# Stores of the RWKV mixers moved to ScalarE's and GpSimd's queues, a shorter first inverse, and later places for the fronts of the chunks

## The chip, the cores and the metric

The kernel runs on one core of one Trainium2 chip. The metric is the time of one execution on the device in microseconds; the median of three runs is taken. Beside the times there is a profile of one execution, which tells for every engine when each instruction ran and what it waited for. The engines are named as the profile names them: PE is TensorE (matrix multiplies; PEld is its loading of weights), DVE is VectorE, ACT is ScalarE, POOL is GpSimd, and SP is SyncE, which here does nothing but issue DMAs. ACT and POOL can issue DMAs too, from the same queue of instructions in which their arithmetic stands.

## The reference, cut to what matters

One inference step of two layers over 1048 tokens (16 meta tokens, 1024 prompt tokens, 8 decode tokens), model width 1024, all in float32. Layer 0 is a Conformer convolution and an MLP; layer 1 is an RWKV-7 mixer and an MLP. The mixer makes six mixtures of each token with the one before it, projects them, and runs a recurrence per head of 64:

```python
r = (xr @ w_r); k = (xk @ w_k); v = (xv @ w_v)
w_log = -softplus(-(w0 + tanh(xw @ w1) @ w2)) - 0.5
decay = exp(-exp(w_log));  a = sigmoid(a0 + (xa @ a1) @ a2);  g = sigmoid(xg @ g1) @ g2
# per head, token after token:
sa = einsum('bhvk,bhk->bhv', S, -kk_t)
S = S * w_t + sa[..., None] * (kk_t * a_t) + v_t[..., None] * k_t
y = einsum('bhvk,bhk->bhv', S, r_t)
# then a norm per head, the bonus (r * k * r_k) * v, the gate g, and @ w_o
```

## The kernel before, in words

The kernel goes through layer 0 first, then the mixer of layer 1, then its MLP. This case is about the mixer.

*Groups and places.* The tokens are cut into four groups (`G1`: 272, 256, 256 and 264 tokens). `mixer_in(g)` goes over the model width in eight places `p` of 128 channels each. At each place PE projects `r`, the small gates `l_g`, `l_w`, `l_a` and `v`, and, one place late, the keys `k` of the next group; ACT copies the results out of PSUM and applies the nonlinear functions, DVE makes from them the operands of the recurrence (`ab`). Before the places, `gate` and `decay_rate` multiply the whole group by narrow weights (`p_g`, `p_wa`, L943 and L944), and `tail` ends the last place of the group before.

*Through DRAM.* What one part makes and another reads in another layout goes through DRAM: the keys (`d_k`), the gates (`d_g`), the operands of the recurrence (`d_ab`), the values with tokens on the partitions (`d_v`), the small matrices to be inverted (`d_n`) and their inverses (`d_p`), the bonus (`d_bv`) and the recurrence's outputs (`d_y`). Before the change SP's queue issues nearly all these stores, and all loads of weights and operands as well.

*Chunks.* The recurrence is computed in chunks of 64 tokens: chunk 0 holds the 16 meta tokens, chunks 1 to 16 the prompt, four for each group. `inverses(c, n)` (L1139 on) inverts small triangular matrices of 32 rows for `n` chunks at once on DVE: it loads `ni` from `d_n`, does 30 steps of one multiply and one add (L1151, L1152), and stores to `d_p`. It is run once for chunk 0 and once for each group's four chunks, during the next group. `front(c)` loads a chunk's operands, makes `A`, the products within the chunk, and transposes the loaded inverse on DVE (`x32`, L1203). `chunk(c)` goes on with the small products `gg`, `W`, `po`, `U`, `S` and `Y` on PE and updates the state `sv`.

*What sets the order.* The program is traced in order; a planner then orders the instructions of each engine by its own estimate, but not PE's: inside `manual_schedule` PE runs in the order in which the program was traced. So PE waits at an instruction whose input is late, even where later ones could run. Inverses and chunks are Python generators. The mixer calls `tick(g)` seven times at each place (five times in group 3). Each call takes one step of the current inverse (`invert`), adds 2.0 to a credit in groups 1 to 3 and runs the recurrence until its yields (costs, in `RW`) have used the credit up (`advance`), and takes one step of the norm of the first output group. A chunk may begin when `st["inv"]` says that its inverse has been traced. `step(c + 1)` lets the next chunk's front run within a chunk, for no credit, if its inverse has been traced.

*Behind the mixers* come the output projection and MLP of the first output group (`mixer_out`, `mlp`). They are traced with what is left of the recurrence, the decode step and the remaining norms as fill, called some 208 times. The last chunk transposes its state on PE (`pfs`, L1310) and stores it.

Of the kernel before, what the change touches and what calls it, by code (L numbers as in the profile page):

```python
# [16 lines left out]
P = 128  # L17
# [3 lines left out]
META = 16  # L21
# [6 lines left out]
HS = 64  # L28
# [17 lines left out]
HALF = [slice(0, HS), slice(HS, P)]  # L46


def hybrid_step(tc, x_prompt, x_sample, state_conv, state_shift, state_wkv, meta_tokens,
# [8 lines left out]
    nc = tc.nc  # L58
    ctx = ExitStack()
    with ctx:  # L60
# [16 lines left out]
        d_k = dram.tile([P, KT, T], F32, name="d_k")  # L77
        d_ab = dram.tile([NCH, P, KT, 2, 2 * HS], F32, name="d_ab")
        d_v = dram.tile([NCH * HS, D], F32, name="d_v")
# [790 lines left out]
        def keys(g, fill):  # L870

            c0, n = G1[g]
            nm = lambda s, *a: f"{s}{g}" + "".join(f"_{x}" for x in a)
            mix = prep[g][0]
            act = [mix(2, k) for k in range(KT)]
            pn = bank(nm("pn"), "x")
            add_pn = lambda: None

            def to_pn(p, sq):
                return lambda: nc.tensor.matmul(pn[:, :n], head_sel(p), sq[:, :n], start=p == 0, stop=p == KT - 1)  # L880
            for p in range(KT):
                yield
                ps = proj(next(wrkv), act, n, nm("k", p), fill)
                k_ = pr.tile([P, N1], F32, name=nm("st", p), tag="st", bufs=2)
                nc.scalar.copy(k_[:, :n], ps[:, :n])
                nc.sync.dma_start(d_k[:, p, c0:c0 + n], k_[:, :n])
                sq = pr.tile([P, N1], F32, name=nm("sq", p), tag="rk", bufs=2)
                nc.scalar.activation(sq[:, :n], ps[:, :n], AF.Square, scale=vec("k_k", p))
                add_pn()
                add_pn = to_pn(p, sq)  # L890
            r16 = lorap.tile([P, N1], F32, name=nm("r16"), tag="lf")
            r16p = norm[g] = [lorap.tile([P, N1], F32R, name=nm("r16" + q), tag="r16" + q, bufs=2)[:, :n] for q in "hl"]
            add_pn()
            nc.vector.tensor_scalar(r16[:, :n], pn[:, :n], L2_EPS * L2_EPS, None, op0=ALU.max)
            nc.scalar.activation(r16[:, :n], r16[:, :n], AF.Sqrt)
            nc.vector.reciprocal(r16[:, :n], r16[:, :n])
            split(*r16p, r16[:, :n], nc.vector)
        carry = {"tail": lambda: None}

        def mixer_in(g, tick):  # L900
# [51 lines left out]
            def decay_rate(ws):  # L952
                ps = narrow(ws, "wa")
                nc.scalar.activation(lwa[0][HALF[0], :n], ps[HALF[0]], AF.Tanh)
                nc.scalar.copy(lwa[1][HALF[1], :n], ps[HALF[1]])
# [23 lines left out]
            wg, ww = narrow_w(1, "g"), narrow_w(0, "wa")  # L979
            act = mixed(0)  # L980
            gate(wg)
            decay_rate(ww)
            carry["tail"]()
            act_v = mixed(3)
            r16p = norm.pop(g)
# [2 lines left out]
            def finish(p, rk, ab, vv):  # L988
                def trace():
                    for s in segs:  # L990
                        if s[3] == HS:
                            nc.sync.dma_start(d_ab[s[0], :, p].rearrange("c r i x -> r c (i x)"),
                                              ab[:, s[4]:s[4] + s[2]].rearrange("r c i t -> r c (i t)"))
                        else:
                            nc.sync.dma_start(d_ab[0, :, p].rearrange("r i (j t) -> r (i j) t", j=2)[:, :, :s[3]],
                                              ab[:, s[4], :, :s[3]])

                    pv_ = bank(nm("vt", p))
                    vt = pr.tile([P, 2, P], F32, name=nm("vt", p), tag="vt")
                    pieces = [(i, a0 + i * P, P) for i in range(ncg // 2)] + ([(2, 0, META)] if g == 0 else [])  # L1000
                    for i, c1, w in pieces:
                        nc.tensor.transpose(pv_[:w, i * P:(i + 1) * P], vv[:, c1:c1 + w], ident)
                    fs_ = slice(p * P, (p + 1) * P)
                    nc.scalar.copy(vt[:, :2].rearrange("p i x -> p (i x)"), pv_[:, :2 * P])
                    nc.sync.dma_start(d_v[ch0 * HS:(ch0 + ncg) * HS, fs_].rearrange("(i t) x -> t i x", t=P), vt[:, :2])
                    if g == 0:
                        vm = pr.tile([P, 2, P], F32, name=nm("vm", p), tag="vt")
                        nc.scalar.copy(vm[:META, 0], pv_[:META, 2 * P:3 * P])
                        nc.sync.dma_start(d_v[:META, fs_], vm[:META, 0])

                    n32 = pr.tile([P, 5, 32], F32, name=nm("n32", p), tag="n32", bufs=2)
                    if g == 0:
                        nc.gpsimd.memset(n32[:, 4], 0.0)
                    pn_ = bank(nm("nn", p))
                    for c in range(ncg):
                        for q in range(2):
                            for j in range(2):
                                o, js = 64 * q + 32 * j, slice(32 * j, 32 * j + 32)
                                nc.tensor.matmul(pn_[o:o + 32, c * 32:(c + 1) * 32], ab[HALF[q], c, 2, js], ab[HALF[q], c, 0, js],
                                                 start=True, stop=True, tile_position=(64 * q, o))  # L1020
                    nc.vector.tensor_mul(n32[:, :ncg], pn_[:, :ncg * 32].rearrange("p (c t) -> p c t", t=32),
                                         nmask.unsqueeze(1).broadcast_to([P, ncg, 32]))
                    if g == 0:
                        pm = bank(nm("nm", p))
                        tok = [slice(64 * q, 64 * q + META) for q in range(2)]
                        for q, o in enumerate(tok):
                            nc.tensor.matmul(pm[o, :META], ab[HALF[q], 4, 2, :META], ab[HALF[q], 4, 0, :META],
                                             start=True, stop=True, tile_position=(64 * q, 64 * q))
                        for o in tok:
                            nc.vector.tensor_mul(n32[o, 4, :META], pm[o, :META], nmask[o, :META])  # L1030
                    nc.sync.dma_start(d_n[ch0:ch0 + ncg, p].rearrange("c r t -> r c t"), n32[:, :ncg])
                    if g == 0:
                        nc.sync.dma_start(d_n[0, p], n32[:, 4])
                    pb = bank(nm("pk", p))
                    nc.tensor.matmul(pb[:, :n], hsum, rk[:, :n], start=True, stop=True)
                    bv = t_("bv", p, "bv", 2)
                    nc.vector.tensor_mul(bv[:, :n], vv[:, :n], pb[:, :n])
                    return lambda: nc.sync.dma_start(d_bv[:, p, c0:c0 + n], bv[:, :n])
                return trace

            def fetch(p):
# [5 lines left out]
            for p, rk2 in ahead_of(fetch):  # L1047
                both()
                ps = proj(next(wrkv), act, n, nm("r", p), both)
                nc.scalar.copy(rk2[:, 2, :n], ps[:, :n])  # L1050
                if npr < n:
                    dd(p, 4, rk2[:, 2, npr:n])
                ps = lora2(wg2, p, lg, f"g{p}")
                gt = t_("gt", p, "gt", 2)
                nc.scalar.copy(gt[:, :n], ps[:, :n])
                nc.sync.dma_start(d_g[:, p, c0:c0 + n], gt[:, :n])

                wa = pr.tile([P, 3, N1], F32, name=nm("wa", p), tag="wa", bufs=2)
                nav, am, cum = (wa[:, i, :] for i in range(3))
# [80 lines left out]
        def inverses(c, n):  # L1140


            B = n * 32
            blocks = lambda d: d[c:c + n].rearrange("c k (e s) t -> (c k e) s t", s=32)
            ni = wk.tile([P, 32, 32], F32, name=f"ni{c}", tag="ni")[:B]
            nc.sync.dma_start(ni, blocks(d_n))
            yield 5
            for j in range(30, 0, -1):
                wd = 31 - j
                o = wk.tile([P, 256], F32, name=f"tt{c}_{j}", tag="tt")[:B, :j * wd].rearrange("p (s t) -> p s t", t=wd)  # L1150
                nc.vector.tensor_mul(o, ni[:, :j, j:j + 1].broadcast_to([B, j, wd]), ni[:, j:j + 1, j + 1:].broadcast_to([B, j, wd]))  # L1151
                nc.vector.tensor_add(ni[:, :j, j + 1:], ni[:, :j, j + 1:], o)  # L1152
                if j % 4 == 0:
                    yield 1.5
            nc.gpsimd.memset(ni.rearrange("p s t -> p (s t)")[:, 0:1024:33], 1.0)
            nc.sync.dma_start(blocks(d_p), ni)
            yield 1
            st["inv"] = c + n - 1

        RW = [4.0, 2.4, 3.12, 5.0, 5.0, 1.28, 3.12, 0.8, 3.0]  # L1160
# [54 lines left out]
        def chunk(c):  # L1215
# [67 lines left out]
            if c > 0:  # L1283
# [10 lines left out]
                nc.scalar.copy(flat(yt), py)  # L1294
                t0 = META + (c - 1) * HS
                for q in range(2):
                    nc.sync.dma_start(d_y[t0:t0 + HS].rearrange("t (k q v) -> q t k v", q=2, v=HS)[q], yt[HALF[q]])

            fs = w_([P, KT, HS], "fs", c, "w1")
            nc.vector.tensor_mul(fs, kv(ps), wend.broadcast_to([P, KT, HS]))  # L1300
# [2 lines left out]
                    nc.vector.tensor_add(sv[HALF[q], :, q, :], fs[HALF[q]], sw[HALF[q]])  # L1303
            else:
                nc.vector.tensor_add(fs, fs, sw)
                fo = w_([P, KT, HS], "fo", c, "sw")
                pt = bank("pfs", "w")
                for p in range(KT):
# [332 lines left out]
```

## Time and profile before

| | us |
|---|---|
| median of three runs | 2875.47 |
| lowest and highest | 2875.14 and 2879.01 |
| the profiled execution | 2871.15 |
| its span, first to last instruction | 2869.4 |
| mean granted clock of PE | 0.967 |

How to read it: the profile gives the busy time of each engine, and for each idle stretch the instruction that ended it. A wait is written as the waiting instruction, an arrow, and what released it: an engine with the tile and the line, or a DMA with what it carried. "x" is a count. In a timeline the columns are start and duration in microseconds, engine, line, operation, tiles, shape. In a table of stages a stretch is given with its length, the busy time of each engine with its number of instructions, the granted clock of PE, and the busy share and rate of the DMA engines. SP's own rows are issues of DMAs: their duration is the time that the queue was taken up by issuing, not that of the transfer. The mixers of groups 0 to 3 lie between about 1163 and 1878 us of the span.

### The profile page before, as it was taken

What the parts mean: (1) busy time and instruction counts of PE and PEld (TensorE: products, weight loads), DVE (VectorE), ACT (ScalarE), POOL (GpSimd) and SP (SyncE); (2) the same over time, 40 slices, a digit from 0 to 9 for tenths busy, and PEclk for the clock granted to TensorE, in tenths of its full rate; (3) what the DMA queues carried; (4) which work ended last, traced back from release to release, by engine and by line L of the source; (5) the groups of instructions that cost most, each with busy time, mean ns of one, the idle gap of its engine ahead of it and who ended that gap; (6) DMA issues with size and microseconds to landing.
All of it is one profiled execution on the core that took longest, in us unless ns stands there. A gap on an engine that the chain in (4) does not pass through costs nothing.

```text
span 2869.4 us, 51630 instructions
## 1 busy us (share of the span) xinstructions
PE 2672.5 (93%) x19594; PEld 2526.5 (88%) x19594; DVE 1799.4 (63%) x3618; ACT 1188.2 (41%) x2235; POOL 1433.1 (50%) x1983
## 2 busy tenths in 40 slices
PE   8999999999999899996998897987889999999998
PEld 7999999999999898885786786877889999999998
DVE  5999999995455545345656464477995554443444
ACT  5545444544354342332454453445444453222223
POOL 6677878987788774000010010154658773333332
PEclk9999999999999999998999899988999999999999
DMA  6663544454445643676677566776665542222221
GB/s 175 178 185 90 153 136 132 138 179 135 139 130 162 183 139 105 192 215 170 173 172 203 140 180 156 179 199 152 175 195 171 170 144 83 67 74 67 67 60 41
DMA packets 651959, 416.43 MB, mean 145 GB/s; under 512 B 126440, under 2 KB 600616, under 8 KB 651710
## 3 DMA queue, kind: packets, MB, share of 16 engines
q1 hardware_dynamic: 645468, 410.20, 50.6%
q10 hardware_dynamic: 6018, 2.89, 0.4%
q8 instruction: 155, 2.54, 0.4%
q14 instruction: 94, 0.77, 0.1%
q0 software_dynamic: 224, 0.03, 0.0%
HBM read 345.60 MB, written 68.37 MB: 144 GB/s over the span
## 4 chain that ended last, share of the span: by engine, by line
PE 72%; DVE 12%; DMA 6%; POOL 3%; issue 3%; ACT 3%; SPq 0%; DVEq 0%; ACTq 0%; POOLq 0%
PE out L187 7%; PE out L189 7%; PE out L188 7%; PE ps_in L187 7%; PE ps_in L189 7%; PE ps_in L188 7%; PE pk L865 4%; PE pv L865 3%; PE pr L865 3%; DVE cv L519 1%; POOL wo_lo L162 1%; DVE tt L1151 1%; POOL wi_lo L162 1%; DVE ni L1152 1%; PE A L1189 1%
## 5 line engine op out<-in xcount | busy, mean ns | idle before, releaser
L162 POOL TENSOR_TENSOR wo_lo<-wo_raw,wo_hi 128x256 fp32r<-128x256 f32 x736 | 563.8, 798 | 274.0 <-ACT wo_hi L157 267.5
L162 POOL TENSOR_TENSOR wi_lo<-wi_raw,wi_hi 128x256 fp32r<-128x256 f32 x640 | 487.2, 793 | 294.8 <-ACT wi_hi L157 290.9
L187 PE MATMUL out<-hh,wo_hi 128*128 128x352 f32 (+2 forms) x1536 | 504.5, 328 | 25.7 <-DVE h L355 14.4
L355 DVE TENSOR_TENSOR h<-h,out 128x352 f32<-128x352 f32 (+2 forms) x768 | 387.4, 510 | 196.6 <-PE out L189 196.1
L189 PE MATMUL out<-hl,wo_hi 128*128 128x352 f32 (+2 forms) x1536 | 495.6, 325 | 7.5 <-DVE hl L141 7.5
L187 PE MATMUL ps_in<-m_h,wi_hi 128*128 128x352 f32 (+2 forms) x1536 | 495.2, 323 | 1.7 <-DVE h L355 1.7
L188 PE MATMUL out<-hh,wo_lo 128*128 128x352 f32 (+2 forms) x1536 | 496.6, 323 | 0.0
L189 PE MATMUL ps_in<-m_l,wi_hi 128*128 128x352 f32 (+2 forms) x1536 | 494.0, 322 | 1.2 <-DVE m_l L285 1.2
L188 PE MATMUL ps_in<-m_h,wi_lo 128*128 128x352 f32 (+2 forms) x1536 | 492.1, 321 | 0.0
L519 DVE SCALAR_TENSOR_TENSOR cv<-u,wdw,cv 128x352 f32<-128x352 f32 (+2 forms) x720 | 376.4, 572 | 0.7
L157 ACT CAST wi_hi<-wi_raw 128x1024 fp32r<-128x1024 f32 x160 | 168.0, 1050 | 393.6 <-PE out L189 200.2
L187 PEld LDWEIGHTS out<-hh,wo_hi 128*128 128x128 f32 x1536 | 293.8, 191 | 32.7 <-DVE h L355 17.2
L157 ACT CAST wo_hi<-wo_raw 128x1024 fp32r<-128x1024 f32 x184 | 192.6, 1049 | 306.2 <-PE out L189 154.3
L189 PEld LDWEIGHTS out<-hl,wo_hi 128*128 128x128 f32 x1536 | 292.6, 191 | 9.5 <-DVE hl L141 9.4
L188 PEld LDWEIGHTS out<-hh,wo_lo 128*128 128x128 f32 x1536 | 293.0, 191 | 0.7
L187 PEld LDWEIGHTS ps_in<-m_h,wi_hi 128*128 128x128 f32 x1536 | 289.8, 189 | 3.5 <-issue 2.2
L189 PEld LDWEIGHTS ps_in<-m_l,wi_hi 128*128 128x128 f32 x1536 | 288.5, 188 | 2.6 <-DVE m_l L285 1.8
L188 PEld LDWEIGHTS ps_in<-m_h,wi_lo 128*128 128x128 f32 x1536 | 288.8, 188 | 1.0
L342 DVE SCALAR_TENSOR_TENSOR r<-ps_in,rs_m 128x352 f32<-128x352 f32 (+2 forms) x192 | 98.2, 514 | 238.1 <-PE ps_in L189 234.5
L141 DVE TENSOR_TENSOR hl<-s,hh 128x352 fp32r<-128x352 f32 (+2 forms) x192 | 147.4, 769 | 108.0 <-ACT hh L140 107.8
L344 ACT ACTIVATE s<-r 128x352 f32<-128x352 f32 (+2 forms) x192 | 93.8, 491 | 134.7 <-DVE r L342 131.6
L865 PE MATMUL pv<-mx,wv_raw 128*128 128x256 f32 (+2 forms) x512 | 126.3, 395 | 8.2 <-ACT rk L1050 6.8
(350 smaller groups left out, 4810.6 us busy)
## 6 DMA issues: line engine op xcount, KB each, us to landing
wi_raw<-in_w_mlp_in_dram SPq DMA_DIRECT2D x160, 512.0 KB
wo_raw<-in_w_mlp_out_dram SPq DMA_DIRECT2D x160, 512.0 KB
wk_raw<-in_rwkv_w_k_dram SPq DMA_DIRECT2D x32, 512.0 KB
wr_raw<-in_rwkv_w_r_dram SPq DMA_DIRECT2D x32, 512.0 KB
wv_raw<-in_rwkv_w_v_dram SPq DMA_DIRECT2D x32, 512.0 KB
d_ab<-ab SPq DMA_DIRECT2D x32, 512.0 KB
pg_raw<-in_conv_w_pw_dram SPq DMA_DIRECT2D x24, 512.0 KB
pa_raw<-in_conv_w_pw_dram SPq DMA_DIRECT2D x24, 512.0 KB
```

The source lines that it names most:

```text
L141: eng_lo.tensor_sub(lo, src, hi.bitcast(F32))
L157: nc.scalar.copy(hi[:, :a * b], raw[:, :a * b])
L162: eng_lo.tensor_sub(lo[:, cs], raw[:, cs], hi[:, cs].bitcast(F32))
L187: nc.tensor.matmul(ps, w[0], act[0], start=first, stop=False)
L188: nc.tensor.matmul(ps, w[1], act[0], start=False, stop=False)
L189: nc.tensor.matmul(ps, w[0], act[1], start=False, stop=last)
L342: nc.vector.scalar_tensor_tensor(r[:, :n], ps[:, :n], 0.0, rs()[:, :n], op0=ALU.max, op1=ALU.mult)
L344: nc.scalar.activation(s[:, :n], r[:, :n], AF.Square)
L355: nc.vector.tensor_add(hv[:, 4 * i + m, :], hv[:, 4 * i + m, :], ps[:, :n])
L519: nc.vector.scalar_tensor_tensor(acc[m][:, :n], ug[:, m, j:j + n], wdw[:, m, j:j + 1], acc[m][:, :n], op0=ALU.mult, op1=ALU.add)
L865: nc.tensor.matmul(ps[:, :n], w[:, k, :], act[k], start=k == 0, stop=k == KT - 1)
L1151: nc.vector.tensor_mul(o, ni[:, :j, j:j + 1].broadcast_to([B, j, wd]), ni[:, j:j + 1, j + 1:].broadcast_to([B, j, wd]))
```

## The change: what it does

1. In the mixers the stores of `d_k`, `d_v`, `d_g` and `d_y` are issued by ACT, those of `d_ab`, `d_n`, `d_bv` and `d_p` by POOL. SP keeps the loads (and, elsewhere in the kernel, the stores that it had).
2. `decay_rate`, the multiplication by the second narrow weight, is traced after the `r` projection of place 0 instead of ahead of `tail`.
3. The inverse of chunk 0 takes 14 steps over 16 rows instead of 30 over 32.
4. `inverses` yields 3 times (chunk 0) or 7 times (the others) after its store, instead of once, before it sets `st["inv"]`.
5. The last chunk yields once more ahead of the transposes of its state.

```diff
@@ keys
-                nc.sync.dma_start(d_k[:, p, c0:c0 + n], k_[:, :n])
+                nc.scalar.dma_start(d_k[:, p, c0:c0 + n], k_[:, :n])
@@ mixer_in
             gate(wg)
-            decay_rate(ww)
             carry["tail"]()
@@ mixer_in, finish (the stores of d_ab, the second of d_v, both of d_n likewise)
-                            nc.sync.dma_start(d_ab[s[0], :, p].rearrange("c r i x -> r c (i x)"),
+                            nc.gpsimd.dma_start(d_ab[s[0], :, p].rearrange("c r i x -> r c (i x)"),
...
-                    nc.sync.dma_start(d_v[ch0 * HS:(ch0 + ncg) * HS, fs_].rearrange("(i t) x -> t i x", t=P), vt[:, :2])
+                    nc.scalar.dma_start(d_v[ch0 * HS:(ch0 + ncg) * HS, fs_].rearrange("(i t) x -> t i x", t=P), vt[:, :2])
...
-                    return lambda: nc.sync.dma_start(d_bv[:, p, c0:c0 + n], bv[:, :n])
+                    return lambda: nc.gpsimd.dma_start(d_bv[:, p, c0:c0 + n], bv[:, :n])
@@ mixer_in, the places
                 nc.scalar.copy(rk2[:, 2, :n], ps[:, :n])
+                if p == 0:
+                    decay_rate(ww)
...
-                nc.sync.dma_start(d_g[:, p, c0:c0 + n], gt[:, :n])
+                nc.scalar.dma_start(d_g[:, p, c0:c0 + n], gt[:, :n])
@@ inverses
-            for j in range(30, 0, -1):
-                wd = 31 - j
+            top = META if c == 0 else 32
+            for j in range(top - 2, 0, -1):
+                wd = top - 1 - j
...
-                nc.vector.tensor_add(ni[:, :j, j + 1:], ni[:, :j, j + 1:], o)
+                nc.vector.tensor_add(ni[:, :j, j + 1:top], ni[:, :j, j + 1:top], o)
                 if j % 4 == 0:
                     yield 1.5
             nc.gpsimd.memset(ni.rearrange("p s t -> p (s t)")[:, 0:1024:33], 1.0)
-            nc.sync.dma_start(blocks(d_p), ni)
-            yield 1
+            nc.gpsimd.dma_start(blocks(d_p), ni)
+            for _ in range(3 if c == 0 else 7):
+                yield 1
             st["inv"] = c + n - 1
@@ chunk
-                    nc.sync.dma_start(d_y[t0:t0 + HS].rearrange("t (k q v) -> q t k v", q=2, v=HS)[q], yt[HALF[q]])
+                    nc.scalar.dma_start(d_y[t0:t0 + HS].rearrange("t (k q v) -> q t k v", q=2, v=HS)[q], yt[HALF[q]])
...
                 nc.vector.tensor_add(fs, fs, sw)
+                yield RW[7] + 3
                 fo = w_([P, KT, HS], "fo", c, "sw")
```

More of the change, by code (lines that the diff above doesn't have):

```diff
@@ L991, in trace @@
                         if s[3] == HS:
-                            nc.sync.dma_start(d_ab[s[0], :, p].rearrange("c r i x -> r c (i x)"),
+                            nc.gpsimd.dma_start(d_ab[s[0], :, p].rearrange("c r i x -> r c (i x)"),
                                               ab[:, s[4]:s[4] + s[2]].rearrange("r c i t -> r c (i t)"))
                         else:
-                            nc.sync.dma_start(d_ab[0, :, p].rearrange("r i (j t) -> r (i j) t", j=2)[:, :, :s[3]],
+                            nc.gpsimd.dma_start(d_ab[0, :, p].rearrange("r i (j t) -> r (i j) t", j=2)[:, :, :s[3]],
                                               ab[:, s[4], :, :s[3]])
@@ L1008, in trace @@
                         nc.scalar.copy(vm[:META, 0], pv_[:META, 2 * P:3 * P])
-                        nc.sync.dma_start(d_v[:META, fs_], vm[:META, 0])
+                        nc.scalar.dma_start(d_v[:META, fs_], vm[:META, 0])
                     n32 = pr.tile([P, 5, 32], F32, name=nm("n32", p), tag="n32", bufs=2)
@@ L1030, in trace @@
                             nc.vector.tensor_mul(n32[o, 4, :META], pm[o, :META], nmask[o, :META])
-                    nc.sync.dma_start(d_n[ch0:ch0 + ncg, p].rearrange("c r t -> r c t"), n32[:, :ncg])
+                    nc.gpsimd.dma_start(d_n[ch0:ch0 + ncg, p].rearrange("c r t -> r c t"), n32[:, :ncg])
                     if g == 0:
-                        nc.sync.dma_start(d_n[0, p], n32[:, 4])
+                        nc.gpsimd.dma_start(d_n[0, p], n32[:, 4])
                     pb = bank(nm("pk", p))
@@ L1147, in inverses @@
             yield 5
-            for j in range(30, 0, -1):
-                wd = 31 - j
+            top = META if c == 0 else 32
+            for j in range(top - 2, 0, -1):
+                wd = top - 1 - j
                 o = wk.tile([P, 256], F32, name=f"tt{c}_{j}", tag="tt")[:B, :j * wd].rearrange("p (s t) -> p s t", t=wd)
-                nc.vector.tensor_mul(o, ni[:, :j, j:j + 1].broadcast_to([B, j, wd]), ni[:, j:j + 1, j + 1:].broadcast_to([B, j, wd]))
-                nc.vector.tensor_add(ni[:, :j, j + 1:], ni[:, :j, j + 1:], o)
+                nc.vector.tensor_mul(o, ni[:, :j, j:j + 1].broadcast_to([B, j, wd]), ni[:, j:j + 1, j + 1:top].broadcast_to([B, j, wd]))
+                nc.vector.tensor_add(ni[:, :j, j + 1:top], ni[:, :j, j + 1:top], o)
                 if j % 4 == 0:
```

## The prediction

> **What bounds the kernel now.** I read the page's busy times first, then busy time by stage, then who waited for whom, then the timeline around the longest waits. The page says that TensorE carries the time:
>
> ```profile
> span 2869.4 us, 51630 instructions
> PE 2672.5 (93%) x19594; PEld 2526.5 (88%) x19594; DVE 1799.4 (63%) x3618; ACT 1188.2 (41%) x2235; POOL 1433.1 (50%) x1983
> ```
>
> So time is won only where PE sits idle. The stages tell where. The first four stretches are the mixers of groups 0 to 3, the fifth is what follows them; the last three are pieces inside the mixers of groups 1, 2 and 3:
>
> ```profile
> core 0: us, PE busy (x) PEld busy (x) DVE busy (x) ACT busy (x) POOL busy (x), PEclk, DMA share, GB/s
> 1176.00:1295.00 119.00, 117.28 (x771) 97.06 (x770) 50.48 (x122) 45.36 (x137) 6.06 (x21) 1.00 0.75 209
> 1295.00:1509.00 214.00, 182.05 (x1870) 153.25 (x1869) 129.41 (x327) 86.31 (x226) 17.44 (x33) 0.93 0.68 172
> 1509.00:1717.00 208.00, 179.63 (x1930) 150.75 (x1929) 115.51 (x265) 95.59 (x236) 18.17 (x32) 0.93 0.67 173
> 1717.00:1878.00 161.00, 140.11 (x1357) 118.30 (x1357) 77.49 (x194) 63.73 (x176) 20.32 (x61) 0.95 0.66 167
> 1878.00:2170.00 292.00, 243.07 (x2503) 226.47 (x2501) 247.72 (x498) 137.97 (x275) 172.49 (x207) 0.91 0.67 182
> ...
> 1405.00:1505.00 100.00, 96.89 (x1181) 82.22 (x1182) 57.13 (x127) 51.87 (x132) 10.88 (x20) 0.98 0.73 180
> 1600.00:1735.00 135.00, 131.01 (x1549) 110.87 (x1547) 70.38 (x148) 68.33 (x171) 14.25 (x26) 1.00 0.71 180
> 1798.00:1850.00 52.00, 52.00 (x639) 43.54 (x639) 24.53 (x57) 24.98 (x71) 9.41 (x28) 0.98 0.69 176
> ```
>
> Groups 1 to 3 leave PE idle for 31.9 + 28.4 + 20.9 = 81.2 us. Yet the three pieces, with the same projections and chunks, run at 97 to 100% busy: no engine is short there, so the idle time is a few waits:
>
> ```profile
> PE gg L1227 <- DVE x L1203: 49.2, 4, 19.3
> PE p_wa L943 <- DMA wa_raw<-d_lr: 9.8, 2, 5.7
> PE pv L865 <- ACT rk L1050: 6.8, 4, 4.0
> PE pfs L1310 <- DVE fs L1305: 5.8, 1, 5.8
> ```
>
> Four waits for `x32`, the transposed inverse, make 49.2 of the 81.2. PE's order is written by hand: `gg` of the first chunk after each inverse stands at a fixed call of `tick`, and PE gets there before the inverse is back from DRAM. The waits of chunks 0, 5 and 9, with the ends of the inverses of 0 and 5:
>
> ```profile
> 1367.36 1.06 PE L1227 MATMUL gg<-x,no 32*32 32x32 f32 x32 [19.27 <-DVE x L1203]
> 1590.32 1.07 PE L1227 MATMUL gg<-x,no 32*32 32x32 f32 x32 [14.77 <-DVE x L1203]
> 1591.32 1.97 PE L1250 MATMUL bT<-ident,bk 128*128 128x128 f32 x8
> 1593.08 3.53 PE L865 MATMUL pr<-mx,wr_raw 128*128 128x256 f32 x10
> 1795.13 1.06 PE L1227 MATMUL gg<-x,no 32*32 32x32 f32 x32 [13.52 <-DVE x L1203]
> ...
> 1330.08 0.17 DVE L1151 TENSOR_TENSOR tt<-ni 32x30 f32<-32x30 f32 x1
> 1330.79 0.20 DVE L1151 TENSOR_TENSOR tt<-ni 32x58 f32<-32x58 f32 x1
> 1360.23 0.18 DVE L1152 TENSOR_TENSOR ni<-ni,tt 32x30 f32<-32x30 f32 x1
> 1538.17 0.19 DVE L1151 TENSOR_TENSOR tt<-ni 128x30 f32<-128x30 f32 x1
> 1584.06 0.19 DVE L1152 TENSOR_TENSOR ni<-ni,tt 128x30 f32<-128x30 f32 x1
> 1589.73 0.45 DVE L1203 STREAM_TRANSPOSE x<-p 128x256 f32<-128x256 f32 x1 [5.48 <-DMA p<-d_p]
> ```
>
> In the second, PE stops at 1575.55 (1590.32 less 14.77), DVE, which began the inverse at 1538.17, ends it at 1584.25, and the way to DRAM and back takes 5.48.
>
> **The change, part by part.**
>
> *Later fronts.* I counted the calls from the code (the yields of `inverses`, 2.0 credits a call, the costs in `RW`). `st["inv"]` was set at calls 10 and 19 of group 1 and call 10 of groups 2 and 3; it will be set at 8 and 23, and at 16. So `gg` of chunk 0 moves from call 14 to 12, of chunk 1 from 25 to 27, of chunks 5 and 9 from 14 to 20. One call without chunk work is about 2.1 us of PE (56 calls in the 119 us of group 0). Chunks 5 and 9 get 6 x 2.1 = 12.7 us of projections ahead of `gg`, work that now follows it; 14.77 and 13.52 shrink to 2.1 and 0.8. Chunk 1, 1.7 before (49.2 less the other three), goes to 0.
>
> *First inverse over 16 rows.* 28 DVE instructions for 60; none is wider than 56 elements, so each takes 0.17 to 0.20: 5.3 us. Before:
>
> ```profile
> L1151 DVE TENSOR_TENSOR tt<-ni 128x30 f32<-128x30 f32 (+19 forms) x150 | 59.2, 395 | 21.9 <-DMA ni<-d_n 18.3
> L1152 DVE TENSOR_TENSOR ni<-ni,tt 128x30 f32<-128x30 f32 (+19 forms) x150 | 55.6, 371 | 3.9
> ```
>
> Five inverses, 114.8 us, 23 each. 17.7 us fall away, two calls (4.2) are given up: 19.27 becomes 5.8 at worst. The tail, which stores the inverse's input, also no longer stands behind `p_wa` (its wait alone was 5.7): I take 2. The four waits leave 5 of 49.2: **-44.2**.
>
> *`decay_rate` behind the first `r` projection.* The loads of `wa_raw` get the tail and 16 matmuls more, about 5 us, which covers waits of 5.7 and 4.1 to within half a microsecond: -9.4. PE now goes from `p_wa` to `l_w` with one small matmul group between, while ACT writes `lwa`: 0.8 x 4 groups, an estimate by half the mean wait at `pv` above (6.8 over 4), +3. The next `hx` load waits for `p_wa`, which moves by the 5 us gained: no cost. Net **-6.4**.
>
> *The clock after a wait.* After 14.77 us of idling, gg, bT and ten projections took 1.07 + 1.97 + 3.53 = 6.6. The same elsewhere:
>
> ```profile
> 1406.65 2.32 PE L865 MATMUL pk<-mx,wk_raw 128*128 128x256 f32 x10
> ...
> 1826.17 0.69 PE L1227 MATMUL gg<-x,no 32*32 32x32 f32 x32
> 1826.79 1.09 PE L1250 MATMUL bT<-ident,bk 128*128 128x128 f32 x8
> ...
> 2133.82 1.97 PE L1310 MATMUL pfs<-ident,fs 64*64 64x64 f32 x32 [5.77 <-DVE fs L1305]
> ```
>
> The first three rows make 4.1, so with their overlaps some 2.2 us are lost. Five waits go (three for `gg`, two for `p_wa`): **-11**.
>
> *The yield before `fo`.* It puts 3.8 credits of MLP between `fs` and its transposes, about 3.8 calls at some 2.8 us (91 calls, by the count, from 1878 to the last row above), more than the wait: -5.8 and its clock, **-8**.
>
> *Stores on ACT.* Their issue on SP, ns least/median/most:
>
> ```profile
> L886 SPq DMA_DIRECT2D d_k<-st x32: 338/764/2067, 1140.5 to 1727.0; - x32
> L1056 SPq DMA_DIRECT2D d_g<-gt x32: 319/522/2579, 1185.0 to 1876.1; - x32
> L1005 SPq DMA_DIRECT2D d_v<-vt x32: 359/370/1225, 1199.7 to 1891.1; - x32
> L1009 SPq DMA_DIRECT2D d_v<-vm x8: 322/322/328, 1204.2 to 1324.8; - x8
> L1297 SPq DMA_DIRECT2D d_y<-yt x32: 514/625/1412, 1430.5 to 2134.5; - x32
> ```
>
> By medians 24.4 + 16.7 + 11.8 + 2.6 + 20.0 = 75.5 us of ACT's own time, behind which the PSUM copies stand that PE's banks wait for. Bounds: 0 and 75.5. What ACT can lose without PE noticing, group 0 shows:
>
> ```profile
> ACT vm L1008 <- DMA d_v<-vt: 39.4, 7, 7.2
> ```
>
> ACT stood still for 39.4 us in those 119, and PE lost 1.7. ACT is busy for 246 of the 583 us of groups 1 to 3. I take a tenth, **+8**. SP without stores can load earlier; as almost no wait on a weight load is seen, I count nothing for it.
>
> *Stores on GpSimd.* 117 (`d_ab` 40, `d_n` 40, `d_bv` 32, `d_p` 5). The only DMAs of POOL before are small loads at the start:
>
> ```profile
> L445 POOL DMA_DIRECT2D stg<-in_norm_mlp_dram x1: 682/682/682, 1.7 to 1.7; - x1
> DMA to landing us min/median/max: 1.7/7.0/7.1
> ```
>
> At 0.7 each they are 80 us on an engine that is busy for 56 of 583, so POOL holds; `ex` and `sw` stand behind them and have a place's time. On the path is only `d_p`: out and back is 5.48, which 1.7 or 7.1 to landing would move by about -1 or +4.4 per inverse: -4 to +18 for four. I take **+2**, near the quiet row.
>
> *Work pushed out.* By the same count chunk 11 is done at the mixers' end before and only begun after: 0.6 chunk goes to the stretch of 1878 to 2170, where DVE is busy for 247.72 of 292. PE's work is the same in either place; some 6 us of DVE's are bounded by 0 and 6: **+3**.
>
> Sum: -44.2 - 6.4 - 11 - 8 + 8 + 2 + 3 = -56.6. The profiled execution took 2871.15, so 2814.5; the median of the runs, 2875.47, stands 4.3 higher, so **2819**.
>
> **Rivals.**
>
> *DVE takes over.* Without the waits, DVE must do 23 us of inverse beside its places: 1538 to 1584 went to one inverse. Six calls bring 12.7 x 0.42 (DVE's share in group 0) = 5.4 us of other DVE work, and if that is mixed in, `x32` comes as much later, and scans and `ab` behind it, so that PE waits at `nn` and `pv` instead. For: the stretch before each wait; 6.8 us at `pv`. Against: DVE is busy for 48 to 60% of groups 1 to 3. Half of the 47.5 of `gg` and `nn` comes back: 2819 + 24 = 2843.
>
> *`d_p` comes late from POOL.* Each inverse's store stands behind those of two places (six at 0.7) and lands in 7.1 instead of half of 5.48: 4.2 + 4.4, some 9 us on four chains, +36, 2855. The Trainium skill (SBUF — State Buffer, Summary: rules for kernel authors) speaks for it: it says to issue a DMA that should hide under VectorE's work from ACT or SP, as GpSimd's descriptor writing starves while VectorE runs its 2x or 4x modes. No run here shows that yet; the 1.7 us landing at 65 us speaks against a fixed price.
>
> *Slower: ACT's queue.* Each store waits for the copy that it stores and then issues, with the next PSUM copy behind it. PE's order is fixed, so it cannot step around. Without the ACT term the change gains 64.6; at 64.6 / 136 = 0.48 us of PE time per store that is gone. At 0.8 each, 109 us, the time is 2920. For: up to 2.6 us for one issue. Against: group 0.
>
> *Nothing.* If the waits only move on to the next fixed matmul, which the 97% pieces speak against, 2875.
>
> **How the numbers follow.** Forecast 0.70, DVE 0.12, POOL 0.06, ACT 0.10, nothing 0.02. Low end: ACT and work pushed out at 0, `gg` at 0, `d_p` at its lower end: 2819 - 8 - 3 - 5 - 4 = 2799. High end: past both faster rivals, 2858. Beyond 0.2% (5.8 us, about what three runs can tell from no change) faster: 0.70 + 0.12 + 0.06 = 0.88; within: 0.02; slower: 0.10.
>
> **What would show it.** Right: `gg` waits for `x` under 10 us in all, no wait on `wa_raw` or `fs`, groups 1 to 3 at 95% busy, the mixers some 60 us shorter, the stretch behind them about equal. Wrong: PE waits on ACT (`rk`, `vv`, `st`) of over 30 us in total; `x` still behind `d_p`; `nn` waiting for `ab`.

## The result, and the profile after

| | before | after |
|---|---|---|
| median, us | 2875.83 (4 runs) | 2831.18 (4 runs) |
| lowest and highest | 2875.14 and 2879.01 | 2823.53 and 2831.85 |
| span of the profiled execution | 2869.4 | 2821.8 |

The ratio is 0.9837, with a 95% interval of 0.9818 to 0.9855: 44.65 us faster, where 56.6 was forecast (2831 for 2819). The profiled execution of after is its fastest run, 7.7 below the median. From the page of after:

```profile
span 2821.8 us, 51604 instructions
PE 2669.5 (95%) x19594; PEld 2521.3 (89%) x19594; DVE 1785.4 (63%) x3586; ACT 1189.5 (42%) x2235; POOL 1520.2 (54%) x2100
```

PE does the same work and stands still for less of the span. The stages of both kernels follow, cut at the same work: the mixers of groups 0, 1, 2 and 3 (each from its first `p_g`), then from the first to the last output projection, then the rest. Before:

```profile
1165.60:1295.20 129.60, 127.88 (x817) 105.81 (x816) 53.21 (x125) 48.52 (x142) 6.06 (x21) 1.00 0.73 205
1295.20:1511.10 215.90, 183.39 (x1874) 154.11 (x1873) 129.41 (x327) 87.52 (x229) 17.44 (x33) 0.93 0.69 172
1511.10:1725.20 214.10, 185.73 (x1957) 155.90 (x1956) 118.87 (x272) 96.46 (x239) 18.28 (x33) 0.93 0.67 174
1725.20:1897.70 172.50, 142.94 (x1509) 120.21 (x1507) 85.16 (x212) 71.35 (x197) 25.57 (x67) 0.93 0.66 167
1897.70:2283.60 385.90, 343.53 (x3045) 328.78 (x3045) 293.89 (x578) 176.44 (x319) 257.11 (x320) 0.94 0.63 176
2283.60:2869.40 585.80, 573.03 (x3587) 568.95 (x3585) 269.21 (x480) 184.92 (x309) 244.53 (x319) 0.99 0.26 78
```

After:

```profile
1161.70:1296.90 135.20, 130.06 (x817) 106.85 (x816) 53.32 (x125) 49.03 (x142) 31.30 (x58) 0.99 0.65 197
1296.90:1496.30 199.40, 180.26 (x1811) 151.36 (x1810) 114.11 (x294) 89.19 (x229) 34.38 (x58) 0.97 0.74 188
1496.30:1699.20 202.90, 185.91 (x2022) 155.23 (x2021) 116.80 (x273) 95.05 (x239) 39.29 (x60) 0.97 0.71 189
1699.20:1840.50 141.30, 129.86 (x1301) 108.37 (x1299) 78.31 (x192) 65.77 (x181) 40.33 (x90) 0.96 0.70 190
1840.50:2233.20 392.70, 354.11 (x3253) 337.98 (x3253) 301.21 (x597) 182.12 (x334) 262.31 (x323) 0.94 0.62 175
2233.20:2821.80 588.60, 575.29 (x3584) 570.52 (x3584) 270.87 (x481) 185.14 (x310) 246.99 (x321) 0.99 0.26 77
```

- The four mixers went from 732.1 to 678.8 us, 53.3 less. Length less busy time, summed, is PE's idle time: 92.2 before, 52.7 after, 39.5 less. The other 13.8 is busy time, by a higher granted clock in groups 1 to 3 and by matmuls that moved on.
- The matmuls that moved are in the fifth stretch, which has 208 more (3045 to 3253). It is 6.8 us longer: PE is busy there for 10.6 us more and idle for 3.8 less (42.4 to 38.6). The last stretch is 2.8 longer.
- Over the whole span PE's busy time fell by only 3.0 us, its idle time by 44.6. What was won is idle time.
- Group 0 alone got longer, by 5.6 us.
- The mixers begin 3.9 us earlier in this execution. In the profiles of all the kernels below they begin between 1161.7 and 1168.8, so this cannot be put down to the change.

Who waited for whom on PE in groups 1 to 3, after (total, times, longest; the smaller rows are left out, but for `wa_raw`):

```profile
PE pb L756 <- ACT vv L1067: 8.2, 4, 3.1
PE l_w L964 <- ACT lw L954: 6.3, 1, 6.3
PE pn L880 <- ACT sq L888: 4.0, 2, 3.0
PE nn L1018 <- DVE ab L1105: 3.6, 1, 3.6
PE gg L1230 <- ACT no L1198: 3.0, 6, 0.7
PE pv L865 <- ACT rk L1049: 2.7, 2, 1.9
...
PE p_wa L943 <- DMA wa_raw<-d_lr: 0.6, 2, 0.4
```

and, in the stretch behind them:

```profile
PE pfs L1314 <- DVE fs L1308: 0.5, 1, 0.5
```

No `gg` waits for `x32` any more; 49.2 us of waits are gone, and nearly all of those on `wa_raw` and `fs` with them. In their place stand shorter ones, none over 6.3 us, most of them for ACT: PE's waits for ACT's tiles in groups 1 to 3 sum to 29.0 us, where they were 18.2 before. One of these takes up a wait that went: group 1's `p_wa` waited 5.65 before; now, in the same group, `l_w` waits 6.31 for ACT's `lw`, which is made from `p_wa`:

```profile
1323.56 1.22 PE L964 MATMUL l_w<-lw,wa 128*128 128x256 f32 x2 [6.31 <-ACT lw L954]
```

### The profile page after: what moved, and what is told of

It reads as the page before. It is cut to its first block, busy times and chain, and to the rows that moved or that the text cites. A ratio compares the mean times of both kernels' runs of the same rounds, so it can differ in the third digit from the quotient of the medians.

```text
span 2821.8 us, 51604 instructions
## 1 busy us (share of the span) xinstructions
PE 2669.5 (95%) x19594; PEld 2521.3 (89%) x19594; DVE 1785.4 (63%) x3586; ACT 1189.5 (42%) x2235; POOL 1520.2 (54%) x2100
## 4 chain that ended last, share of the span: by engine, by line
PE 71%; DVE 13%; DMA 6%; issue 4%; ACT 3%; POOL 2%; SPq 0%; ACTq 0%; DVEq 0%; POOLq 0%
PE ps_in L187 8%; PE ps_in L189 8%; PE ps_in L188 8%; PE out L187 8%; PE out L189 8%; PE out L188 8%; PE pk L865 3%; PE pr L865 2%; PE pv L865 2%; POOL wo_lo L162 1%; DVE ni L1154 1%; DVE cv L519 1%; PE ps_o L189 1%; DVE tt L1153 1%; PE ps_o L188 1%
## 5 line engine op out<-in xcount | busy, mean ns | idle before, releaser
L141 DVE TENSOR_TENSOR hl<-s,hh 128x352 fp32r<-128x352 f32 (+2 forms) x192 | 147.1, 767 | 106.2 <-ACT hh L140 106.0
```

The source lines that it names most:

```text
L141: eng_lo.tensor_sub(lo, src, hi.bitcast(F32))
```

## The experiments

The theory was that of the prediction: most of the gain is the waits for `x32`, the moved stores cost some 10 us, the rest is as its terms say. Its rivals were that the queues themselves are the gain, that the yields or the first inverse do nothing, and that `decay_rate` is a term of its own. Each kernel is compared with the kernel before on the same chip; "against the change" is its median less 2831.2. The kernel before was run again on each chip, with medians of 2875.0, 2875.2 and 2877.2, so these differences are good to some 2 us at best.

**The stores alone, and all but the stores.** The first puts only the 253 moved stores into the kernel before; the second puts them back on SP in the changed kernel.

```diff
-                nc.sync.dma_start(d_k[:, p, c0:c0 + n], k_[:, :n])
+                nc.scalar.dma_start(d_k[:, p, c0:c0 + n], k_[:, :n])
...
-            nc.sync.dma_start(blocks(d_p), ni)
+            nc.gpsimd.dma_start(blocks(d_p), ni)
```

> The kernel before with nothing but the stores moved to ScalarE's and GpSimd's queues. By my sum the moved stores cost 10 us (8 on ACT, 2 on POOL), the four waits of gg for x stay at about 49 us: some 10 us slower than before. By the rival, that a freed SP brings loads earlier and that this is where the gain is from: at least 25 us faster, with the waits of p_wa for wa_raw and of pv for rk gone.

> The changed kernel with all stores back on SP: fronts later, first inverse over 16 rows, decay_rate moved, yield before fo. By my sum it is 10 us faster than the changed kernel, some 55 us faster than before. By the rival that the queues matter: about 20 us faster than before, with waits of gg for x of 15 us or more left, as p32 comes late behind the stores.

The stores alone: 2892.58, ratio 1.0063 (1.0046 to 1.0080), 17.5 us slower. All but the stores: 2816.46, ratio 0.9795 (0.9780 to 0.9809), 58.6 us faster than before and 14.7 faster than the change. Both ways the stores cost 15 to 18 us; the rival that the queues are the gain falls. Groups 1 to 3 with the stores alone:

```profile
1293.00:1519.80 226.80, 188.35 (x1874) 158.21 (x1874) 129.75 (x327) 90.17 (x231) 35.65 (x60) 0.90 0.65 163
1519.80:1743.40 223.60, 188.46 (x1958) 157.62 (x1957) 119.29 (x272) 96.93 (x239) 35.05 (x58) 0.91 0.63 168
1743.40:1920.20 176.80, 144.14 (x1509) 120.93 (x1508) 85.56 (x212) 71.74 (x197) 42.83 (x94) 0.92 0.63 165
```

PE is idle there for 106.2 us, against 90.4 before, and the clock is lower. The waits of the same kernel say what was late:

```profile
PE gg L1227 <- DVE x L1203: 55.5, 4, 19.8
...
PE pv L865 <- ACT rk L1050: 7.8, 4, 4.9
...
PE pb L756 <- ACT vv L1066: 6.7, 2, 3.6
```

The inverses come later (55.5 for 49.2) and so does what ACT makes (14.5 for 8.8).

**One queue back at a time.** The changed kernel with ACT's stores, then with POOL's, on SP again. One store of each is shown.

```diff
-                nc.scalar.dma_start(d_g[:, p, c0:c0 + n], gt[:, :n])
+                nc.sync.dma_start(d_g[:, p, c0:c0 + n], gt[:, :n])
```

```diff
-            nc.gpsimd.dma_start(blocks(d_p), ni)
+            nc.sync.dma_start(blocks(d_p), ni)
```

> The changed kernel with ACT's stores (d_k, d_v, d_g, d_y) back on SP, those of POOL left there. The moved stores together cost some 14 us in the changed kernel. By my sum four fifths of that are ACT's issues ahead of the PSUM copies: 11 us faster than the changed kernel. By the rival that POOL's way to DRAM is what costs: the same as the changed kernel within 4 us.

> The changed kernel with POOL's stores (d_ab, d_n, d_bv, d_p) back on SP, those of ACT left there. By my sum 3 us faster than the changed kernel. By the rival that d_n and d_p land late from POOL (5.3 us at the median for d_p in the changed kernel): 10 us or more faster, with the inverses ending earlier.

ACT's back: 2821.01, 0.9814 (0.9785 to 0.9843), 10.2 faster than the change. POOL's back: 2826.56, 0.9825 (0.9807 to 0.9843), 4.6 faster. Both are on the forecast side and add up to the 14.7, but each interval overlaps the change's, so the total is shown and its split only likely. The waits of one execution each point the same way for ACT: those for ACT's tiles in groups 1 to 3 sum to 22.7 us with ACT's stores back on SP and 22.6 with all of them back, where the change has 29.0. What an issue costs the engine, after, in ns (least/median/most):

```profile
L886 ACTq DMA_DIRECT2D d_k<-st x32: 326/327/500, 1135.6 to 1697.7; - x32
L1057 ACTq DMA_DIRECT2D d_g<-gt x32: 326/327/357, 1181.5 to 1822.4; - x32
L991 POOL DMA_DIRECT2D d_ab<-ab x32: 754/754/864, 1196.7 to 1834.8; - x32
```

The d_k and d_g stores are shorter on ACT than the prediction took from SP (764 and 522), and steadier.

**The fronts back.** The changed kernel with one yield after each inverse, as before.

```diff
-            for _ in range(3 if c == 0 else 7):
+            for _ in range(1 if c == 0 else 1):
                 yield 1
```

> The changed kernel with the later fronts undone alone: one yield after the inverse's store, as before. By my sum gg waits again for chunks 5 and 9, about 13 us each, and for chunk 1 by some us, with 2.2 us of slow clock after each: 30 us slower than the changed kernel. By the rival that the stores and the shorter first inverse made the inverses come earlier: at most 10 us slower.

2864.88, 0.9961 (0.9946 to 0.9976): 33.7 slower than the change. Three of the waits come back, in this kernel's timeline:

```profile
1392.43 1.06 PE L1230 MATMUL gg<-x,no 32*32 32x32 f32 x32 [8.69 <-DVE x L1206]
1585.95 1.06 PE L1230 MATMUL gg<-x,no 32*32 32x32 f32 x32 [15.60 <-DVE x L1206]
1785.85 1.06 PE L1230 MATMUL gg<-x,no 32*32 32x32 f32 x32 [6.93 <-DVE x L1206]
```

They are those of chunks 1, 5 and 9, 31.2 us in all. Chunk 0, with its shorter inverse, does not wait even without its two further yields.

**The first inverse back to 32 rows.**

```diff
-            top = META if c == 0 else 32
+            top = 32
```

> The changed kernel with the first inverse over all 32 rows again (30 steps). It then also yields seven 1.5 credits instead of three, so st[inv] is set at call 12 and gg of chunk 0 stands four calls later, some 8 us of PE. By my sum 17.7 us of DVE come back: gg of chunk 0 waits for x for about 10 us, with 2.2 us of clock, and the other inverse of that group comes late by as much, but has room: 12 us slower than the changed kernel. By the rival that the first inverse has room enough: the same within 3 us.

2846.18, 0.9892 (0.9870 to 0.9914): 15.0 slower than the change, with the wait of chunk 0 back, and 1.5 of chunk 1:

```profile
1373.86 1.07 PE L1230 MATMUL gg<-x,no 32*32 32x32 f32 x32 [11.44 <-DVE x L1206]
```

The longer inverse also yields more often, so that this `gg` stands later than in the change: PE gets to it 61.0 us after the group's first `p_g`, where it took 53.8 in the change. Without that the wait would be longer.

**The yield before `fo` taken out.**

```diff
-                yield RW[7] + 3
```

> The changed kernel without the last chunk's extra yield. By my sum pfs waits for fs again, 5.8 us and 2.2 of clock: 8 us slower than the changed kernel. By the rival that PE's wait there only moves on to the next matmul that DVE feeds: the same within 2 us.

2832.76, 0.9856 (0.9835 to 0.9876): 1.6 from the change, within what can be told apart. The wait on `fs` was 3.4 there, not 5.8, and the yield hides all but 0.5 of it; the time does not show it. The prediction had 8 us for it.

**`decay_rate` back ahead of the tail.**

```diff
             gate(wg)
+            decay_rate(ww)
             carry["tail"]()
...
-                if p == 0:
-                    decay_rate(ww)
```

> The changed kernel with decay_rate back ahead of tail. By my sum 6.4 us of wait and 4.4 us of clock come back: 11 us slower than the changed kernel. By the rival that the wait for lw (6.3 us at l_w in group 1 of the changed kernel) takes the place of the wait for wa_raw: the same time within 3 us, l_w waits for nothing and p_wa for 6 to 10 us.

2860.65, 0.9942 (0.9925 to 0.9959): 29.5 slower than the change, where 11 was expected. All four fronts wait for their inverses again:

```profile
1353.61 1.06 PE L1229 MATMUL gg<-x,no 32*32 32x32 f32 x32 [5.85 <-DVE x L1205]
1394.47 0.47 PE L1229 MATMUL gg<-x,no 32*32 32x32 f32 x18 [1.54 <-DVE x L1205]
1593.15 1.06 PE L1229 MATMUL gg<-x,no 32*32 32x32 f32 x32 [8.90 <-DVE x L1205]
1796.47 1.06 PE L1229 MATMUL gg<-x,no 32*32 32x32 f32 x32 [5.62 <-DVE x L1205]
```

Together 21.9 us of waits are back. So without the move the later fronts and the first inverse leave 21.9, and not the 5 that the prediction left (the stores, which alone had added 6.3 to these waits, are moved here too). In chunk 5, PE gets to `gg` 82.5 us after the group's first `p_g`, 18.1 later than before the change, but `x32` is ready 12.2 later too. Of these 12.2 us, 8.0 are the inverse itself, which took DVE 54.1 us here (46.1 before, 45.8 in the change):

```profile
1530.35 0.19 DVE L1152 TENSOR_TENSOR tt<-ni 128x30 f32<-128x30 f32 x1
...
1584.22 0.19 DVE L1153 TENSOR_TENSOR ni<-ni,tt 128x30 f32<-128x30 f32 x1
```

The planner mixes DVE's other work into an inverse in a new way with each edit, so no edit here moves one thing alone.

The theory had to be changed: the place of `decay_rate` is above all a place in the inverse's chain. The tail stores the last of the inverse's input, and it stood behind `p_wa`. The first `p_g` of group 2 and SP's load of the inverse's input, before:

```profile
1511.11 0.59 PE L943 MATMUL p_g<-hx,g_raw 128*128 128x256 f32 x2
...
1533.00 0.59 SPq L1146 DMA_DIRECT2D ni<-d_n  x1
```

and after:

```profile
1496.27 0.59 PE L943 MATMUL p_g<-hx,g_raw 128*128 128x256 f32 x2
...
1508.77 0.33 SPq L1147 DMA_DIRECT2D ni<-d_n  x1
```

From the one to the other it took 21.9 us before and 12.5 after, 9.4 less. The moved stores do not make this difference: it is 12.7 with the move alone and all stores on SP, and 23.1 with the stores moved and `decay_rate` back. The prediction had taken 2. Two kernels tested this reading: `decay_rate` back, but the fronts later still, which should bring the time back although `p_wa` waits; and the move of `decay_rate` alone in the kernel before.

```diff
-            for _ in range(3 if c == 0 else 7):
+            for _ in range(5 if c == 0 else 11):
```

> The changed kernel with decay_rate ahead of the tail again and the fronts later still: 5 yields for chunk 0 and 11 for the others, for 3 and 7. Theory: with decay_rate back (2860.7, 29.5 slower than the change) 20 of the 29.5 were waits at gg for inverses that came later, as the tail stands behind p_wa. Four calls of some 2.1 us cover 8.4 us of each of the waits of 8.9, 5.6 and 1.5, two calls 4.2 of the 5.9 of chunk 0: 2 us of waits for x32 stay, with the clock some 23 us come back, less 3 for work pushed out: 2841. Rival: decay_rate's place costs by itself (its weights' load, PE's order around it), and the late inverses were a sign of it only: the waits go, but the time stays at 2855 to 2863.

> The kernel before with decay_rate behind the first r projection and nothing else changed. Theory: p_wa's waits of 9.8 us go, and the inverses come some 6 to 12 us earlier against gg, so that the waits for x32 fall from 49 to 25 to 30; with the clock 30 us less, 5 lost in group 0: 2850. Rival (the prediction's own term: p_wa alone, with its clock): 11 us less, 2864, gg as long as before.

With later fronts: 2830.07, 0.9833 (0.9815 to 0.9852). All of the 29.5 came back, 11 more than expected, and the time is the change's, though `p_wa` still waits. The rival, that the place costs by itself, falls. Two of its waits:

```profile
PE p_wa L943 <- DMA wa_raw<-d_lr: 5.4, 1, 5.4
...
PE gg L1229 <- DVE x L1205: 3.3, 1, 3.3
```

So no gain from taking the wait on `wa_raw` away is seen. Where it stands, the kernel does without the 5 us of group 0 (130.0 us here) and without the 6.3 at `l_w`. But its fronts are later than the change's as well, so the wait was not priced alone. The fifth stretch is 399.9 us long, 7.2 longer than in the change; this is work of PE that moved there (busy for 363.0 us, where it was 354.1), not idle time. The move alone: 2855.10, 0.9924 (0.9906 to 0.9941), 22 us faster than before, 5 from the theory's 2850 and 9 from the rival's 2864. Its waits for `x32` bear the theory out (the profile is of its slowest run, 5.3 us above the median):

```profile
1369.61 1.06 PE L1228 MATMUL gg<-x,no 32*32 32x32 f32 x32 [12.98 <-DVE x L1204]
1407.60 0.69 PE L1228 MATMUL gg<-x,no 32*32 32x32 f32 x32 [1.69 <-DVE x L1204]
1586.61 1.06 PE L1228 MATMUL gg<-x,no 32*32 32x32 f32 x32 [8.57 <-DVE x L1204]
1780.92 1.06 PE L1228 MATMUL gg<-x,no 32*32 32x32 f32 x32 [5.97 <-DVE x L1204]
```

Against 19.27, 1.67, 14.77 and 13.52 before, three of the four inverses come 6.2 to 7.6 us earlier against their `gg`; that of chunk 1 does not.

**A better version.** All stores on SP, and `decay_rate` moved in groups 1 to 3 alone; then the same with earlier fronts.

```diff
             gate(wg)
+            if g == 0:
+                decay_rate(ww)
             carry["tail"]()
...
-                if p == 0:
+                if p == 0 and g:
                     decay_rate(ww)
```

> The changed kernel with all mixer stores on SP again, and with decay_rate at its old place in group 0 alone (groups 1 to 3 keep the new one). Theory: with all stores on SP the time was 2816.5; group 0 was 134 to 135 us long in every kernel that had decay_rate behind the first r projection and 130 in every one that had it ahead of the tail, since no wait for wa_raw is there to be hidden in that group; so 4.5 us less, 2812, with group 0 at 130 and groups 1 to 3 unchanged. Rival: the 5 us are work that stands in another stage otherwise, and group 1 gets longer by as much: 2816 to 2817.

```diff
-            for _ in range(3 if c == 0 else 7):
+            for _ in range({0: 1, 1: 5, 5: 7, 9: 6}.get(c, 7)):
```

> The same kernel as with all stores on SP and decay_rate at its old place in group 0, and the fronts of the chunks somewhat earlier: 1 yield for chunk 0, 5 for chunk 1, 6 for chunk 9, for 3, 7 and 7. Theory: x32 stood ready 11, 9 and 7 us before gg in those three, so that no wait comes back, and work that the later fronts pushed behind the mixers comes back into them; of the 3 us that the prediction took for it, 1 to 2: 2810. Rival: the margins are smaller than one execution shows, a wait of a few us at gg comes back with its clock: 2815 to 2820.

The first: 2813.99, 0.9782 (0.9754 to 0.9809), 17.2 faster than the change. Against 0.9795 with `decay_rate` moved in all groups, the time cannot tell the two apart, but the stage can: group 0 with the move in all groups (all stores on SP), and then without it there:

```profile
1167.20:1301.70 134.50, 130.26 (x817) 106.95 (x816) 53.16 (x125) 49.13 (x142) 6.05 (x21) 0.99 0.71 198
```

```profile
1168.80:1298.30 129.50, 127.78 (x816) 105.70 (x816) 53.23 (x125) 48.72 (x142) 6.06 (x21) 1.00 0.73 205
```

Groups 1 to 3 did not get longer for it (543.0 and 537.4 us in all), which the rival asked for. Earlier fronts: 2814.64, 0.9777 (0.9760 to 0.9793): no difference. Waits for `x32` of 3.4 us (chunk 1) and 4.8 (chunk 5) came back, and no time was lost by them. Chunk 5's yields had not been touched, so its margin was as small as the rival said.

## Why the prediction was right, and where it was not

It said faster, 2819 with a range of 2799 to 2858; the time is 2831. The mechanism held: PE waited for late inverses, and the waits went. The gain was forecast 12 us too high, and some terms were wrong in ways that offset each other. By its steps:

- *Later fronts and first inverse (-44.2).* The amount came, not by these two parts. The four waits are gone, 5 us more than forecast. But with `decay_rate` back 21.9 of them stay; the tail's way, put at 2, took the rest. There chunk 0 waits for 5.85, as the sum has it without the tail, but chunks 5 and 9 wait for 8.90 and 5.62 instead of 2.1 and 0.8. In chunk 5 DVE was later with the inverse, as in the rival in which DVE takes over. In chunk 9 PE got to `gg` only 9.0 us later and not 12.7, and the wait of 4.1 for `wa_raw` ahead of it, which had gone, makes up the difference. That none is left is partly luck: chunk 5's `x32` was ready at 1569.10 and its `gg` began at 1569.70, and the same place waited for 1.9 us in the kernel with ACT's stores back. The 5 us that the sum leaves is not exact either: 5.8 - 2 + 2.1 + 0.8 are 6.7 if the tail's 2 us count once. The two parts are worth 33.7 and 15.0 when undone. With the 29.5 of `decay_rate` that is 78, more than the whole gain: all three bring the same `gg` and `x32` apart, so what one is worth depends on the others, and such terms must not be added up from kernels that undo one each.
- *`decay_rate` (-6.4).* The step that failed. The tail's way was taken as 2 us and measured 6.2 to 7.6 for three of the inverses, which makes the 20 of the 49.2 that the move alone takes away. Its own part was no gain: `p_wa`'s waits fell from 9.8 to 0.6, but the 5.65 of group 1 became 6.31 at `l_w` (3 was set for that, in four groups; with all stores on SP it is 3.2 to 3.7). And group 0, where nothing had waited for `wa_raw`, got 5.6 us longer: PE's idle time rose by 3.4 there, and its clock was lowered for 3.4 us.
- *The clock (-11).* Near, as far as it can be told. Time in which PE was busy, weighted with the share of the clock that was missing in the trace, fell from 21.0 to 12.6 us in the mixers, by 8.4. But PE's busy time over the whole span fell by only 3.0, so how much of the 8.4 the kernel's time got is open.
- *The yield before `fo` (-8).* Too high: 1.6, which is nothing measurable. The wait of 5.8, priced whole and with a clock loss on top, was only 3.4 once the rest of the change was there, and 0.5 of it stayed.
- *Stores (+8 and +2).* Too low: 14.7 in all, likely 10.2 of ACT and 4.6 of POOL. By the slower rival's own measure this is 0.075 us of PE time for each of ACT's 136 stores, far from the 0.48 from which the change would lose. By their medians ACT's issues took some 53 us in all, where 75.5 was the bound. The mark of that rival, over 30 us of waits for ACT's `rk`, `vv` and `st`, did not come: `pb` and `pv` waited 8.2 and 2.7. But the rival is right in part: all of ACT's tiles together held PE for 29.0 us in groups 1 to 3, 6.4 more than with all stores on SP.
- *Work pushed out (+3).* About right, for what it priced. The stretch behind the mixers is 6.8 longer, but by PE's own work, which the mixers no longer do. Its idle time, from which the 3 us were to come, rose by 1.5 if the wait on `fs` is left aside (36.6 to 38.1).

Without the stores the terms come to 2809, and all but the stores measured 2816.5; so 5 of the 12 us are the stores and 7 the rest, in which too much gain at `fo` and `decay_rate` was partly made up by the waits for `x32`. The low end of the range is 2 us off: with `d_p` going from +2 to -4 it is 2797. Of the prediction's marks, the waits for `x32`, `wa_raw` and `fs` came out. The mixers are 53.3 us shorter, not 60, and the stretch behind them is not equal but 6.8 longer. Groups 1 to 3 are busy for 91% (496.0 of 543.6), not 95, since PE's fixed order meets the next late operands, above all `vv`, `lw` and `sq` by ACT and `ab` by DVE. The marks of the rival in which DVE takes over, `nn` and `pv`, stayed small over the whole kernel, at 4.1 and 2.7.

*`d_p` late from POOL.* This rival fell: 9 us on four chains did not come. From issue to the start of `x`, chunk 5 in the changed kernel:

```profile
1559.19 0.55 POOL L1158 DMA_DIRECT2D d_p<-ni  x1 [2.86 <-issue]
...
1568.65 0.45 DVE L1206 STREAM_TRANSPOSE x<-p 128x256 f32<-128x256 f32 x1 [1.53 <-DMA p<-d_p]
1569.70 0.97 PE L1230 MATMUL gg<-x,no 32*32 32x32 f32 x26
```

and with all stores on SP:

```profile
1567.27 0.33 SPq L1158 DMA_DIRECT2D d_p<-ni  x1
...
1575.50 0.42 DVE L1206 STREAM_TRANSPOSE x<-p 128x256 f32<-128x256 f32 x1
```

They take 9.5 and 8.2 us, and `gg` does not wait for `x32` in either. With the stores alone, the way from issue to `x` was 0.1 to 2.4 us longer for the four inverses that `gg` waited for than it was before. POOL's `d_p` landed 3.2 to 6.1 us after its issue, which is nearer to the rival's 7.1 than to the quiet row's 1.7; the later fronts had room for it. The Trainium skill (SBUF — State Buffer, Summary: rules for kernel authors), which spoke for this rival, has descriptor writing on GpSimd starve under VectorE's fast modes; no run here shows a delay at `d_p` of that kind.

*Why the stores cost at all.* With the stores alone, PE's largest sum of waits for a load in the mixers, that of `p_wa`, went from 9.8 to 8.8 us: SP's free time brought next to nothing forward that PE waited for. The Trainium skill (DMA: Bandwidth & Descriptors, Issuing engines are not separate DMA queues) says that issuing from several engines saves only the sequencer's issue time. The runs agree in that nothing more was won, and go further: here the saving was worth nothing, and the moved stores cost 14.7 us on engines whose results PE waits for. That it is the issue time itself, and not the longer way of the stores that follow, was not separated.

## What to carry to other kernels

Where an engine runs in a fixed order, follow the late operand's whole chain back (here store, load, inverse, store, load, transpose) and look for work that stands ahead of its first link: moving one block of matmuls behind the tail brought three of four inverses 6 to 8 us forward and was worth 22 us alone, more than twice the wait that it was seen to have (9.8). In this kernel the stores were better left on SP, which makes no operands, than on engines whose results PE waits for; SP was not so late with its loads that it mattered. Parts that hide the same wait cannot be priced one by one.

## What the runs showed that was not expected

- An issue of the same store took 327 ns on ACT at the median where SP took 764 (`d_k`), and hardly varied; POOL took 754 for `d_ab` where SP took 384. Cheaper issues did not make the store cheaper for the kernel.
- Waits of 5.4 us (`p_wa`) and of 3.4 and 4.8 (`gg`) stood in kernels that are as fast as those without them. What took the place of each was not traced one by one; in these kernels the length of such a wait was no measure of what its removal gives.
